# Feeding the first pair of experts: one-hot products of token tiles in SBUF in place of an indirect DMA

## The chip, the cores and the metric

The kernel runs on one core of one Trainium2 chip. The metric is the device time of one execution in microseconds (us), median of three runs. A difference of about 0.2% (3.9 us) is what a measurement of this kernel can tell from no change.

## The reference

Two transformer blocks over 512 tokens of width 1024, all in fp32: feed-forward, mixer, feed-forward, then a second mixer and a mixture of experts. Only the last part is touched by the change:

```python
def hierarchical_moe(h, w_group, b_group, w_expert, b_expert, w_gate, w_up, w_down):
    ...
    g_sel = jnp.argmax(g_logits, axis=-1)               # 1 of 4 groups
    top_vals, top_idx = lax.top_k(e_in, TOP_K)          # 2 of its 8 experts
    weights = g_w[:, None] * jax.nn.softmax(top_vals, axis=-1)
    ...
    def expert_block(args):                             # each expert on its own tokens
        xb, e = args
        hid = jax.nn.silu(xb @ w_gate[e]) * (xb @ w_up[e])
        return hid @ w_down[e]
    ...
    y = jnp.sum(y_buf[dest].reshape(T, TOP_K, D) * weights[..., None].astype(h.dtype), axis=1)
```

There are 32 experts with 1024x512 gate and up matrices and a 512x1024 down matrix each, 192 MiB of weights in all, every byte of which is loaded once.

## The kernel before

The activations stand as eight tiles `xT[d]` of 128 features x 512 tokens. The MoE stage treats the experts as 16 pairs, each expert with 64 slots for tokens, so that a pair's tokens fill 128 columns. A pair needs 12 weight tiles of 1 MiB (`load_experts`, L1247): four for gate, four for up, four for down. All are issued on SP's queue in one fixed order into 18 buffers (`NWA` 9 on the right end of SBUF, `NWB` 9 on the left), so tile 18, the third tile of pair 0's down matrices, goes where pair 0's first gate tile was, and can be issued only when TensorE has read that one for the last time. The order is pair 0 gate, up, pair 1 gate, up, pair 0 down, pair 2 gate, and so on: tiles 18 and 19 wait for the first half of pair 0's gate, 20 and 21 for the second half, 22 to 25 for its up.

While the mixer's last products still run, `route_tile` (L1210) adds up the router's logits feature tile by feature tile, and `token_tile` (L1232) turns `xT[d]` into rows of tokens, four 128x128 transposes for each d, copied by ScalarE into `stage` (a tile `tok` for two d), and stored by a DMA on ScalarE's queue into `rows` in DRAM. `route` (L1313) finds the two experts of each token on VectorE and `pos`, the slot of each token in each expert. `route_weights` (L1355) makes the weights `Wb` from logits; in the list of work it comes later, and the planner mixes its operations into `route`.

`hot` (L1390) makes one-hot matrices `P[b]` (128 tokens x slots, bf16) by comparing slot numbers with `pos`. `fetch` (L1409) multiplies them with token numbers to learn which token sits in which slot, and `fetch_rows` (L1420) gathers those rows from DRAM by an indirect DMA on GpSimd's queue into a `tok` tile. `turned` (L1439) turns the gathered rows back, eight transposes for a pair, and VectorE multiplies with the norm's gain into `xe`. Before any expert runs, pairs 0 and 1 are fetched so.

`experts` (L1452) then runs a pair: `first(0, ..)` is the gate's product, `first(1, ..)` the up's, each of 16 matmuls for four of the eight feature tiles. For pair 0 TensorE's order is written out by hand (L1469 to L1479); for the later ones it is too, over the whole of `experts`:

```python
                self.turned(0, 0)
                first(0, range(4))
                self.turned(0, 1)
                first(0, range(4, 8))
                self.route_weights()
                self.scales(0)
                self.scales(1)
                self.hot(1)
                self.fetch(2)
                first(1, range(8))
```

Each engine works off its queue in order.

Of the kernel before, what the change touches and what calls it, by code (L numbers as in the profile page):

```python
# [7 lines left out]
F32 = mybir.dt.float32  # L8
F32R = mybir.dt.float32r
BF = mybir.dt.bfloat16  # L10
I32 = mybir.dt.int32
AF = mybir.ActivationFunctionType
OP = mybir.AluOpType
# [3 lines left out]
T = 512  # L17
# [252 lines left out]
class Kernel:  # L270
# [119 lines left out]
    def part(self, t, i, c0=0, c1=None):  # L390

        c1 = T - 128 * i if c1 is None else c1
        o = 512 * PART[i] + OFF[i]
        return t[:, o + c0:o + c1]
# [837 lines left out]
    def token_tile(self, d):  # L1232


        nc = self.nc
        if d % 2 == 0:
            self.stage = self.p_tok.tile([128, 4, 256], F32, name="tok", tag="tok")
        pt = self.z([128, 4, 128])
        for b in range(4):
            nc.tensor.transpose(pt[:, b], self.xT[d][:, b * 128:b * 128 + 128], self.ident)  # L1240
        o = 128 * (d % 2)
        nc.scalar.copy(self.stage[:, :, o:o + 128], pt)
        if d % 2:
            to = self.rows.rearrange("(b p) c -> p b c", p=128)[:, :, 128 * d - 128:128 * d + 128]
            nc.scalar.dma_start(to, self.stage)

    def load_experts(self, n):  # L1247

# [20 lines left out]
    def moe_begin(self, st):  # L1269
        nc = self.nc  # L1270
        P = lambda n, b=1, **k: self.pool(st, n, b, **(k or dict(side="right", reuse_waits="tile")))
        self.p_one, self.p_tok = P("one_moe"), P("tok", 3)
        self.fill(self.p_one, 64)
        self.p_we = [P("we_a", NWA)]
        self.we, self.n_we = {}, 0
        self.c_con2 = self.one([128, self.aps["con2"].shape[1]], "c_con2")
        nc.scalar.dma_start(self.c_con2, self.aps["con2"])
        self.w_r = self.wk(288).rearrange("p (d c) -> p d c", d=ND)
        nc.scalar.dma_start(self.w_r, self.aps["w_r"])
        self.b_r = self.one([128, 36], "b_r")  # L1280
        nc.scalar.dma_start(self.b_r, self.aps["b_r"].to_broadcast([128, 36]))
        self.tri = self.one([128, 256], "tri", BF)
        nc.gpsimd.memset(self.tri, 1.0)
        nc.gpsimd.affine_select(self.tri[:, :128], self.tri[:, :128], [[1, 128]], OP.is_gt, 0.0, base=0, channel_multiplier=-1)
        self.top = self.one([128, 4, 8], "top")
        self.tb = self.one([128, 4, 2], "tb", BF)
        nc.vector.tensor_copy(self.tb.rearrange("p b c -> p (b c)"), self.con2("parts"))
        self.rows = P("rows", space=bass.MemoryType.DRAM).tile([T, D], F32, name="rows")
        self.acc = self.p_s1.tile([128, T], F32, name="acc")
        self.pr = self.at([128, 4, 36])  # L1290

    def moe(self, st):
        P = lambda n, b=1: self.pool(st, n, b, reuse_waits="tile")
        self.p_xe, self.p_sel, self.p_o = P("xe", 4), P("sel"), P("oexp")
        self.p_we += reversed([P(f"we_b{i}") for i in range(NWB)])
        self.load_experts(192)
        with self.hp():
            self.route()
        self.ws, self.xg = {}, {}
        with self.hp():  # L1300
            for pr in range(2):
                self.hot(0, 2 * pr, 2)
                self.fetch(pr)
        self.later = None
        for pr in range(16):
            if pr >= MAN:
                with self.tc.manual_schedule(engines={mybir.EngineType.PE}):
                    self.experts(pr)
            else:
                self.experts(pr)  # L1310
        self.overflow()
# [75 lines left out]
        nc.vector.tensor_copy(Wb[:, :, 2:9:3], r)  # L1387
        nc.vector.tensor_copy(self.Wb[:, :, :, 9:], self.tb[:, :, None, :].to_broadcast([128, 4, 16, 2]))

    def hot(self, g, first=0, n=4):  # L1390

        nc = self.nc
        if first == 0:
            self.P = [self.p_sel.tile([128, 256], BF, name=f"P{b}") for b in range(4)]
        s = [128, n, 64]
        for b in range(4):
            e = 4 * g + first
            nc.vector.tensor_tensor(self.P[b][:, 64 * first:64 * first + 64 * n].rearrange("p (e s) -> p e s", e=n),
                                    self.con2("slots")[:, None, :].to_broadcast(s),
                                    self.pos[:, b, e:e + n, None].to_broadcast(s), op=OP.is_equal)  # L1400

    def slots(self, pr, cols, n):

# [5 lines left out]
    def fetch(self, pr):  # L1409

        nc = self.nc
        ws = self.ws[pr] = self.p_sel.tile([128, 32], F32, name="ws", bufs=4)
        p = self.slots(pr, self.tb, 2) if pr < 2 else self.slots(pr, self.Wb[:, :, pr], 11)
        n = 0 if pr < 2 else 9
        nc.vector.tensor_reduce(ws[:, 2:3], p[:, n:n + 2], AX.X, OP.add)
        self.fetch_rows(pr, ws)
        if pr > 1:
            self.scales(pr, p)

# [18 lines left out]

    def turned(self, pr, half):  # L1439

        nc = self.nc
        if half == 0:
            self.xe = []
        p = self.at([128, 4, 128])
        for k in range(4):
            c = 512 * half + 128 * k
            nc.tensor.transpose(p[:, k], self.xg[pr][:, c:c + 128], self.ident)
        t = self.p_xe.tile([128, 4, 128], F32, name="xe", tag="xe")
        nc.vector.tensor_tensor(t, p, self.vec("norm2", 4 * half, 4)[:, :, None].to_broadcast([128, 4, 128]), op=OP.mult)
        self.xe += [t[:, k] for k in range(4)]  # L1450

    def experts(self, pr):  # L1452

        nc = self.nc
# [6 lines left out]
        def first(kind, kk):  # L1461
            for k in kk:
                for e in range(2):
                    c = 512 * (k % 4)
                    mm(gu[kind][64 * e:64 * e + 64], self.xe[k][:, 64 * e:64 * e + 64], w(kind, k // 4, e)[:, c:c + 512],  # L1465
                       start=(k == 0), stop=(k == 7))

        if pr == 0:
            with self.tc.manual_schedule(engines={mybir.EngineType.PE}):  # L1469
                self.turned(0, 0)  # L1470
                first(0, range(4))
                self.turned(0, 1)
                first(0, range(4, 8))
                self.route_weights()
                self.scales(0)
                self.scales(1)
                self.hot(1)
                self.fetch(2)
                first(1, range(8))  # L1479
            self.overflow_count()  # L1480
        else:
            first(0, range(8))
            first(1, range(8))
            if pr < 14:
                self.fetch(pr + 2)
# [65 lines left out]
        if last:  # L1551


            part = lambda: self.p_xe.tile([128, T], F32R, name="xe", tag="xe")
            with self.hp():
                down(0, part(), part(), self.mm())
            v[1] = part(), part()
            held = {d: self.z() for d in range(4, 8)}
            for c in TAIL.split():
                n = int(c[1])  # L1560
# [152 lines left out]
```

## Time and profile before

| | us |
|---|---|
| median of three runs (1925.04 to 1925.8) | 1925.8 |
| the profiled execution: its own time | 1927.15 |
| its span, first to last instruction | 1925.3 |
| PE busy in the span | 1863.8 (97%) |
| DVE, ACT, POOL busy | 901.8, 643.9, 307.7 |
| mean granted TensorE clock | 0.988 |

Times in the rows are us from the span's start. PE is TensorE's matmuls, DVE VectorE, ACT ScalarE, POOL GpSimd, SP the engine on whose queue the weights are issued. The MoE stage is the last quarter, from about 1426 us on.

### The profile page before, as it was taken

The numbers are of one execution on the slowest core, as the hardware profiler recorded it, in microseconds if no ns is written. First come the engines' busy times: TensorE is split into PE (matmuls) and PEld (weight loads), VectorE is DVE, ScalarE is ACT, GpSimd is POOL, SyncE is SP. The second block draws the span as 40 slices with busy tenths as digits, with TensorE's granted clock in tenths as the row PEclk, the third lists the DMA queues.
The fourth block names the chain that finished last, engine by engine and source line by source line (L and its number), as shares of the span: only waits on it lengthen the run. The fifth ranks groups of instructions, "written<-read, shape, count | busy, mean of one in ns | idle before, by whom it ended". The sixth has DMA issues, their size and how long they took to land.

```text
span 1925.3 us, 22975 instructions
## 1 busy us (share of the span) xinstructions
PE 1863.8 (97%) x8605; PEld 1305.7 (68%) x8605; DVE 901.8 (47%) x1734; ACT 643.9 (33%) x1218; POOL 307.7 (16%) x290
## 2 busy tenths in 40 slices
PE   8999999999999999999999999999978999999998
PEld 6888888877666778888888888777762333333333
DVE  5444453344998745444443343456651333343232
ACT  5333333344445734333333333466520100000000
POOL 3322210133021032222320100012120000000000
PEclk9999999999999999999999999999988999999999
DMA  4222232222111122222222222211297999999997
GB/s 155 99 99 97 92 102 99 97 79 71 66 56 44 45 88 99 88 99 99 99 99 98 91 99 90 86 55 54 89 404 290 420 419 420 420 420 419 419 421 282
DMA packets 69185, 330.49 MB, mean 172 GB/s; under 512 B 8784, under 2 KB 11216, under 8 KB 45008
## 3 DMA queue, kind: packets, MB, share of 16 engines
q1 hardware_dynamic: 63648, 321.48, 43.4%
q0 software_dynamic: 2304, 4.20, 0.6%
q10 hardware_dynamic: 3120, 3.32, 0.6%
q8 instruction: 69, 1.13, 0.2%
q14 instruction: 44, 0.36, 0.1%
HBM read 328.97 MB, written 4.19 MB: 173 GB/s over the span
## 4 chain that ended last, share of the span: by engine, by line
PE 60%; DMA 6%; DVE 3%; ACT 2%; issue 1%; POOL 0%; ACTq 0%; POOLq 0%; SPq 0%; DVEq 0%
PE mm L429 11%; PE mm L431 11%; PE mm L430 11%; PE mm L1465 8%; DMA we<-in_w_moe 5%; PE z L1521 4%; PE z L1539 1%; PE z L450 1%; PE z L452 1%; PE z L451 1%; PE z L918 1%; PE z L1538 1%; PE at L1179 1%; PE z L877 1%; DVE wk L1515 1%
## 5 line engine op out<-in xcount | busy, mean ns | idle before, releaser
L252 DVE TENSOR_TENSOR wl<-raw,wh 128x512 fp32r<-128x512 f32 x440 | 347.9, 792 | 442.1 <-ACT wh L251 432.9
L251 ACT CAST wh<-raw 128x512 fp32r<-128x512 f32 x440 | 272.4, 622 | 557.7 <-PE mm L430 468.5
L429 PE MATMUL mm<-xs,wh 128*128 128x512 f32 x1008 | 396.7, 394 | 7.3 <-ACT wh L251 7.3
L431 PE MATMUL mm<-xs,wl 128*128 128x512 f32 x1008 | 394.9, 392 | 1.0 <-DVE wl L252 1.0
L430 PE MATMUL mm<-xs,wh 128*128 128x512 f32 x1008 | 394.8, 392 | 0.6 <-DVE xs L502 0.4
L1465 PE MATMUL mm<-we,xe 128*64 128x512 f32 x1024 | 232.6, 602 | 2.6 <-DMA we<-in_w_moe 1.2
L429 PEld LDWEIGHTS mm<-xs,wh 128*128 128x128 f32 x1008 | 189.6, 188 | 54.2 <-ACT wh L251 7.3
L430 PEld LDWEIGHTS mm<-xs,wh 128*128 128x128 f32 x1008 | 189.6, 188 | 47.5 <-issue 5.7
L431 PEld LDWEIGHTS mm<-xs,wl 128*128 128x128 f32 x1008 | 189.6, 188 | 44.0 <-issue 4.1
L1465 PEld LDWEIGHTS mm<-we,xe 128*64 128x64 f32 x1024 | 73.7, 138 | 148.6 <-issue 136.3
L429 PE MATMUL mm<-hid,wh 128*128 128x512 f32 x352 | 136.9, 389 | 0.0
L430 PE MATMUL mm<-hid,wh 128*128 128x512 f32 x352 | 136.9, 389 | 0.0
L431 PE MATMUL mm<-hid,wl 128*128 128x512 f32 x352 | 136.9, 389 | 0.0
L563 POOL TENSOR_TENSOR wk<-wk 128x512 f32<-128x512 f32 x44 | 69.9, 1591 | 310.1 <-DVE wk L562 292.5
L1521 PE MATMUL z<-we,wk 128*64 128x512 f32 x480 | 113.8, 599 | 2.6 <-DMA we<-in_w_moe 2.3
L1514 ACT ACTIVATE oh<-z,ws 128x512 fp32r<-128x512 f32 x30 | 20.6, 688 | 247.4 <-PE z L1521 247.4
L1493 DVE SCALAR_TENSOR_TENSOR wk<-mm,ws,wk 128x512 f32<-128x512 f32 x16 | 12.0, 751 | 182.0 <-issue 160.6
L513 POOL TENSOR_TENSOR acc<-acc,wd 128x512 f32<-128x512 f32 x34 | 46.5, 1367 | 270.3 <-ACT wd L512 269.6
L1545 DVE TENSOR_TENSOR x<-z,x 128x512 f32<-128x512 f32 x116 | 72.0, 683 | 20.6 <-PE z L1539 20.6
L1426 POOL DMA_INDIRECT tok<-rows,islot x16 | 16.1, 1006 | 388.0 <-DVE islot L1424 324.2
L1521 PEld LDWEIGHTS z<-we,wk 128*64 128x64 f32 x480 | 32.6, 136 | 63.9 <-issue 54.3
L429 PEld LDWEIGHTS mm<-hid,wh 128*128 128x128 f32 x352 | 66.1, 188 | 13.8
(441 smaller groups left out, 2529.8 us busy)
## 6 DMA issues: line engine op xcount, KB each, us to landing
we<-in_w_moe SPq DMA_DIRECT2D x188, 1024.0 KB, 19.9
raw<-in_stream SPq DMA_DIRECT2D x220, 512.0 KB, 3.2
we<-in_w_moe SPq DMA_DIRECT2D x16, 256.0 KB, 9.8
x<-in_xT SPq DMA_DIRECT2D x8, 256.0 KB, 6.0
rows<-tok ACTq DMA_DIRECT2D x4, 512.0 KB
out<-x SPq DMA_DIRECT2D x8, 256.0 KB, 2.3
c_con<-in_con SPq DMA_DIRECT2D x1, 512.0 KB
c_con<-in_con ACTq DMA_DIRECT2D x1, 344.0 KB
```

What stands on the lines that cost most here:

```text
L251: nc.scalar.copy(h, r)
L252: nc.vector.tensor_sub(l, r, h.bitcast(F32))
L429: mm(p, h, xh[k], start=(k == 0), stop=False)
L430: mm(p, h, xl[k], start=False, stop=False)
L431: mm(p, l, xh[k], start=False, stop=(k == n - 1))
L450: mm(pv[b], self.xh[k][:, t], wh, start=(k == 0), stop=False)
L513: nc.gpsimd.tensor_add(self.acc, self.acc, sq)
L563: nc.gpsimd.tensor_mul(u, s, u)
L1465: mm(gu[kind][64 * e:64 * e + 64], self.xe[k][:, 64 * e:64 * e + 64], w(kind, k // 4, e)[:, c:c + 512], start=(k == 0), stop=(k == 7))
L1514: nc.scalar.activation(oh, pd, AF.Copy, scale=ws[:, 0:1])
L1521: mm(p[64 * e:64 * e + 64], ht[:, k * 128 + 64 * e:k * 128 + 64 * e + 64], self.down_rows(w(2, half, e), half, k), start=(k == 0), stop=(k ...
L1545: nc.vector.tensor_add(self.xT[d], p, self.xT[d])
```

## The change

Pair 0 no longer fetches its rows. `token_tile` keeps all four stage tiles in SBUF (`tok` now has four buffers). `hot_first` makes fp32 one-hots `P0[b]` for the first two experts in a `wk` tile; `gather_first` multiplies each 128x128 block of the stage tiles with them, four matmuls (one for each block of tokens) for each of the eight feature tiles, 32 in all, and `gained` takes the place of the second half of `turned`. Pair 0's token numbers are still found (`fetch(0)`, without the DMA), later. Pairs 1 and up are fetched as before. `hot(0)` is made once for four experts. All operations of `route_weights` on VectorE are put behind the last operation of `hot(0)`, and the two `scales` now stand ahead of the gate's second half in TensorE's order. `xe` has two buffers in place of four; the last pair's outputs go to `tok` tiles instead.

```diff
@@ -1234,15 +1234,15 @@
 
         nc = self.nc
         if d % 2 == 0:
-            self.stage = self.p_tok.tile([128, 4, 256], F32, name="tok", tag="tok")
+            self.stage.append(self.p_tok.tile([128, 4, 256], F32, name="tok", tag="tok"))
         pt = self.z([128, 4, 128])
         for b in range(4):
             nc.tensor.transpose(pt[:, b], self.xT[d][:, b * 128:b * 128 + 128], self.ident)
         o = 128 * (d % 2)
-        nc.scalar.copy(self.stage[:, :, o:o + 128], pt)
+        nc.scalar.copy(self.stage[-1][:, :, o:o + 128], pt)
         if d % 2:
             to = self.rows.rearrange("(b p) c -> p b c", p=128)[:, :, 128 * d - 128:128 * d + 128]
-            nc.scalar.dma_start(to, self.stage)
+            nc.scalar.dma_start(to, self.stage[-1])
 
     def load_experts(self, n):
 
@@ -1269,8 +1269,8 @@
     def moe_begin(self, st):
         nc = self.nc
         P = lambda n, b=1, **k: self.pool(st, n, b, **(k or dict(side="right", reuse_waits="tile")))
-        self.p_one, self.p_tok = P("one_moe"), P("tok", 3)
-        self.fill(self.p_one, 64)
+        self.p_one, self.p_tok = P("one_moe"), P("tok", 4)
+        self.fill(self.p_one, 96)
         self.p_we = [P("we_a", NWA)]
         self.we, self.n_we = {}, 0
         self.c_con2 = self.one([128, self.aps["con2"].shape[1]], "c_con2")
@@ -1283,6 +1283,7 @@
         nc.gpsimd.memset(self.tri, 1.0)
         nc.gpsimd.affine_select(self.tri[:, :128], self.tri[:, :128], [[1, 128]], OP.is_gt, 0.0, base=0, channel_multiplier=-1)
         self.top = self.one([128, 4, 8], "top")
+        self.stage = []
         self.tb = self.one([128, 4, 2], "tb", BF)
         nc.vector.tensor_copy(self.tb.rearrange("p b c -> p (b c)"), self.con2("parts"))
         self.rows = P("rows", space=bass.MemoryType.DRAM).tile([T, D], F32, name="rows")
@@ -1291,16 +1292,15 @@
 
     def moe(self, st):
         P = lambda n, b=1: self.pool(st, n, b, reuse_waits="tile")
-        self.p_xe, self.p_sel, self.p_o = P("xe", 4), P("sel"), P("oexp")
+        self.p_xe, self.p_sel, self.p_o = P("xe", 2), P("sel"), P("oexp")
         self.p_we += reversed([P(f"we_b{i}") for i in range(NWB)])
         self.load_experts(192)
         with self.hp():
             self.route()
         self.ws, self.xg = {}, {}
         with self.hp():
-            for pr in range(2):
-                self.hot(0, 2 * pr, 2)
-                self.fetch(pr)
+            self.hot_first()
+            self.hot(0)
         self.later = None
         for pr in range(16):
             if pr >= MAN:
@@ -1387,17 +1387,47 @@
         nc.vector.tensor_copy(Wb[:, :, 2:9:3], r)
         nc.vector.tensor_copy(self.Wb[:, :, :, 9:], self.tb[:, :, None, :].to_broadcast([128, 4, 16, 2]))
 
-    def hot(self, g, first=0, n=4):
-
-        nc = self.nc
-        if first == 0:
-            self.P = [self.p_sel.tile([128, 256], BF, name=f"P{b}") for b in range(4)]
-        s = [128, n, 64]
-        for b in range(4):
-            e = 4 * g + first
-            nc.vector.tensor_tensor(self.P[b][:, 64 * first:64 * first + 64 * n].rearrange("p (e s) -> p e s", e=n),
-                                    self.con2("slots")[:, None, :].to_broadcast(s),
-                                    self.pos[:, b, e:e + n, None].to_broadcast(s), op=OP.is_equal)
+    def hot(self, g):
+
+        nc = self.nc
+        P = []
+        s = [128, 4, 64]
+        for b in range(4):
+            t = self.p_sel.tile(s, BF, name=f"P{b}")
+            last = nc.vector.tensor_tensor(t, self.con2("slots")[:, None, :].to_broadcast(s),
+                                           self.pos[:, b, 4 * g:4 * g + 4, None].to_broadcast(s), op=OP.is_equal)
+            P.append(t.rearrange("p e s -> p (e s)"))
+        self.P = P
+        self.last_hot = last
+
+    def hot_first(self):
+
+        nc = self.nc
+        t = self.wk()
+        s = [128, 2, 64]
+        self.P0 = [t[:, 128 * b:128 * b + 128] for b in range(4)]
+        for b in range(4):
+            nc.vector.tensor_tensor(self.P0[b].rearrange("p (e s) -> p e s", e=2), self.con2("slots")[:, None, :].to_broadcast(s),
+                                    self.pos[:, b, 0:2, None].to_broadcast(s), op=OP.is_equal)
+
+    def gather_first(self, kk):
+
+        nc = self.nc
+        for k in kk:
+            if k % 4 == 0:
+                self.pg = self.at([128, 4, 128])
+            o = 128 * (k % 2)
+            for b in range(4):
+                nc.tensor.matmul(self.pg[:, k % 4], self.stage[k // 2][:, b, o:o + 128], self.P0[b], start=(b == 0), stop=(b == 3))
+            if k % 4 == 3:
+                self.gained(self.pg, k // 4)
+
+    def gained(self, p, half):
+        if half == 0:
+            self.xe = []
+        t = self.p_xe.tile([128, 4, 128], F32, name="xe", tag="xe")
+        self.nc.vector.tensor_tensor(t, p, self.vec("norm2", 4 * half, 4)[:, :, None].to_broadcast([128, 4, 128]), op=OP.mult)
+        self.xe += [t[:, k] for k in range(4)]
 
     def slots(self, pr, cols, n):
 
@@ -1413,7 +1443,8 @@
         p = self.slots(pr, self.tb, 2) if pr < 2 else self.slots(pr, self.Wb[:, :, pr], 11)
         n = 0 if pr < 2 else 9
         nc.vector.tensor_reduce(ws[:, 2:3], p[:, n:n + 2], AX.X, OP.add)
-        self.fetch_rows(pr, ws)
+        if pr:
+            self.fetch_rows(pr, ws)
         if pr > 1:
             self.scales(pr, p)
 
@@ -1438,16 +1469,11 @@
 
     def turned(self, pr, half):
 
-        nc = self.nc
-        if half == 0:
-            self.xe = []
         p = self.at([128, 4, 128])
         for k in range(4):
             c = 512 * half + 128 * k
-            nc.tensor.transpose(p[:, k], self.xg[pr][:, c:c + 128], self.ident)
-        t = self.p_xe.tile([128, 4, 128], F32, name="xe", tag="xe")
-        nc.vector.tensor_tensor(t, p, self.vec("norm2", 4 * half, 4)[:, :, None].to_broadcast([128, 4, 128]), op=OP.mult)
-        self.xe += [t[:, k] for k in range(4)]
+            self.nc.tensor.transpose(p[:, k], self.xg[pr][:, c:c + 128], self.ident)
+        self.gained(p, half)
 
     def experts(self, pr):
 
@@ -1467,13 +1493,17 @@
 
         if pr == 0:
             with self.tc.manual_schedule(engines={mybir.EngineType.PE}):
-                self.turned(0, 0)
+                self.gather_first(range(4))
+                self.fetch(1)
+                self.gather_first(range(4, 5))
                 first(0, range(4))
-                self.turned(0, 1)
-                first(0, range(4, 8))
-                self.route_weights()
+                self.gather_first(range(5, 8))
+                self.fetch(0)
+                with self.tc.issue_after(self.last_hot.ins):
+                    self.route_weights()
                 self.scales(0)
                 self.scales(1)
+                first(0, range(4, 8))
                 self.hot(1)
                 self.fetch(2)
                 first(1, range(8))
@@ -1551,10 +1581,10 @@
         if last:
 
 
-            part = lambda: self.p_xe.tile([128, T], F32R, name="xe", tag="xe")
+            part = lambda: [t[:, i] for t in [self.p_tok.tile([128, 2, T], F32R, name="tok", tag="tok")] for i in range(2)]
             with self.hp():
-                down(0, part(), part(), self.mm())
-            v[1] = part(), part()
+                down(0, *part(), self.mm())
+            v[1] = part()
             held = {d: self.z() for d in range(4, 8)}
             for c in TAIL.split():
                 n = int(c[1])
```

## Rows read from the trace of the kernel before

**Rows 1.** Page, part 2: DMA busy in tenths, 40 slices of 48 us.

```profile
DMA  4222232222111122222222222211297999999997
```

**Rows 2.** Windows: busy us (instructions) by engine, granted clock, DMA share, GB/s.

```profile
1396.00:1442.00 46.00, 37.81 (x223) 32.63 (x221) 27.30 (x86) 13.58 (x25) 10.13 (x8) 0.85 1.02 419
1442.00:1457.50 15.50, 7.31 (x27) 2.96 (x28) 0.72 (x2) 0.00 (x0) 2.22 (x2) 0.58 0.19 57
1457.50:1469.00 11.50, 10.05 (x54) 3.74 (x54) 5.55 (x22) 1.97 (x2) 0.99 (x1) 0.85 0.95 370
1469.00:1472.00 3.00, 3.00 (x18) 1.01 (x14) 0.00 (x0) 0.00 (x0) 0.00 (x0) 1.00 0.56 148
1472.00:1893.00 421.00, 407.01 (x1868) 159.23 (x1862) 138.64 (x287) 36.88 (x58) 12.89 (x13) 1.00 1.01 420
```

**Rows 3.** Waits of PE from 1700 to the end: total us, times, longest.

```profile
PE z L1521 <- DMA we<-in_w_moe: 2.3, 2, 1.3
...
PE mm L1465 <- DMA we<-in_w_moe: 1.2, 1, 1.2
```

**Rows 4.** Timeline of PE: start, us, instruction, count, [idle before, releaser].

```profile
1435.99 1.60 PE L1406 MATMUL z<-tb,P 128*128 128x2 bf16 x8 [0.71 <-DVE P L1398]
1449.40 1.11 PE L1447 MATMUL at<-c_con,tok 128*128 128x128 f32 x4 [11.81 <-DMA tok<-rows,islot]
1451.30 5.54 PE L1465 MATMUL mm<-we,xe 128*64 128x512 f32 x16 [0.78 <-DVE xe L1449]
...
1458.22 3.65 PE L1465 MATMUL mm<-we,xe 128*64 128x512 f32 x16 [0.35 <-DVE xe L1449]
1461.80 0.36 PE L1406 MATMUL z<-Wb,P 128*128 128x9 bf16 x8
...
1464.52 2.02 PE L1465 MATMUL mm<-we,xe 128*64 128x512 f32 x6
```

**Rows 5.** Timeline of SP: the first weight issues after the pause.

```profile
1456.87 0.80 SPq L1261 DMA_DIRECT2D we<-in_w_moe  x2
...
1461.89 0.80 SPq L1261 DMA_DIRECT2D we<-in_w_moe  x2
...
1469.89 0.33 SPq L1261 DMA_DIRECT2D we<-in_w_moe  x1
```

**Rows 6.** Timeline of POOL: the first indirect DMA.

```profile
1444.99 1.23 POOL L1426 DMA_INDIRECT tok<-rows,islot  x1 [15.88 <-DMA rows<-tok]
```

**Rows 7.** Timeline of DVE: routing, one-hots, weights.

```profile
1432.51 0.17 DVE L1365 TENSOR_REDUCE gw<-ge 128x4 f32<-128x16 f32 x1 [1.19 <-ACT ge L1363]
...
1435.32 0.29 DVE L1352 SCALAR_TENSOR_TENSOR pos<-z,ab 128x128 f32<-128x128 f32 x1 [0.21 <-PE z L1349]
1435.64 1.71 DVE L1398 TENSOR_TENSOR P<-c_con,pos 128x128 bf16<-128x128 f32 x8
...
1441.51 0.36 DVE L1387 CAST Wb<-wk 128x192 bf16<-128x192 f32 x1
...
1462.93 1.42 DVE L1398 TENSOR_TENSOR P<-c_con,pos 128x256 bf16<-128x256 f32 x4
```

**Rows 8.** Timeline of PE: 128x128 transposes (L1240) and fp32 products (L1075).

```profile
1388.73 3.15 PE L1075 MATMUL z<-U,R 128*128 128x129 f32 x20
1391.72 2.40 PE L1075 MATMUL z<-V,R 128*128 128x128 f32 x20
...
1429.25 3.65 PE L1240 MATMUL z<-c_con,x 128*128 128x128 f32 x16
```

**Rows 9.** Windows, as rows 2: the granted clock around small products and transposes.

```profile
1388.70:1390.20 1.50, 1.50 (x9) 1.50 (x8) 0.51 (x1) 0.69 (x1) 0.00 (x0) 0.50 0.98 336
1390.40:1391.90 1.50, 1.50 (x16) 1.50 (x15) 0.60 (x2) 0.25 (x2) 0.00 (x0) 1.00 0.01 3
...
1429.00:1433.00 4.00, 3.91 (x19) 3.50 (x18) 2.16 (x16) 1.91 (x5) 0.12 (x1) 0.50 1.03 428
1449.40:1455.00 5.60, 4.81 (x14) 1.95 (x16) 0.69 (x1) 0.00 (x0) 0.00 (x0) 0.50 0.09 34
```

## The prediction

> **What bounds the kernel now.** I read the DMA line of the page first [rows 1]: its last quarter is one block at full share with a notch at its head. Windows cut along that block [rows 2] show the weight stream full from 1396 to 1442 us, nearly idle to 1457.5 (share 0.19), then 0.95 and 0.56 to 1472, and full again, 420 GB/s at a share of 1.01, to 1893. In that last stretch PE is busy 407 of 421 us as well, so the question is which of the two sets the end. The waits of PE from 1700 on [rows 3] answer it: only 3.5 us in all, but for weights. So the stream sets the end, and PE would be ready only some 3.5 us sooner. The idle time of the DMA engines is 0.81 x 15.5 + 0.05 x 11.5 + 0.44 x 3 = 12.6 + 0.6 + 1.3 = 14.5 us, and nothing later gives it back.
>
> Its cause is on PE [rows 4]: it stands still for 11.81 us, until 1449.40, for the gathered rows of pair 0. These were asked for only at 1444.99, since the indirect DMA waited for the store of the rows [rows 6], which lay behind the full stream. All 18 weight buffers are full by then, and the next weights are issued at 1456.87, as the first half of pair 0's gate ends at 1456.84 [rows 4, 5]. The pairs 1461.89 and 1469.89 follow PE in the same manner.
>
> **Part by part.** *Route without weights between.* VectorE stood 1.19 us for an exponential of the weights, then did 0.17 us of them, before the router went on [rows 7]. Behind the last one-hot these are off the path: `pos`, done at 1435.61, comes about 1.2 us sooner, 1434.4. If the planner keeps the gap, this is 0.
>
> *One-hots.* Eight 128x128 took 1.71 us, 0.21 each [rows 7]. Four in fp32: 0.9 us, the first at 1434.7, the last at 1435.3. No row shows a fp32 output of this compare; at the 0.29 of `pos`, also fp32 and 128 wide, it is 0.3 us more, hidden behind the products. The four 128x256 of `hot(0)` take 1.42 us [rows 7] to 1436.7, under PE's products.
>
> *Products.* 16 transposes of 128x128 took 3.65 us at half clock, 0.228 each; 20 fp32 products of the same shape took 2.40 us at full clock, 0.12 each [rows 8, 9]. I price a product so at either clock. The first 16 run from 1434.7 to 1438.4. They read the first two stage tiles, which are copied while the mixer's products still run, and wait for no DMA. Then VectorE's `xe`: from the transposes' end at 1450.51 to the first expert matmul at 1451.30 is 0.79 us [rows 4], so 1439.2; meanwhile PE does the four small matmuls of `fetch(1)` and four products more (0.5 to 0.9 us), to 1439.4. The experts start at 1439.4 in place of 1451.30.
>
> [...]
>
> *Gate, first half.* 16 matmuls took 5.54 us where the clock rose on the way and 3.65 where it was full [rows 4, 9]; all at half clock would be 7.3. So it ends at 1443.05, 1444.95 or 1446.7, against 1456.84. Which it is hangs on the clock. [...]
>
> [...]
>
> *Restart of the stream.* 0.65 us behind that matmul [rows 2, 5]: 1443.7, 1445.6 or 1447.4, against 1457.5. Tiles 18 and 19 take 2.5 us each at 420 GB/s, and pair 1's gather 1.25 us (128 rows of 4 KB, 0.52 MB), to about 1450.0. By then the second half must be through: 12 products 1.45 us, `xe` 0.8 (under it the slots of `fetch(0)` and both `scales`, 0.2 to 0.4 us), 16 matmuls 3.65: 1443.05 + 5.9 = 1448.95. It is, so tiles 20 and 21 follow at once, and the up (3.65 per half, to 1452.6) is again ahead of tile 22. The idle after 1442 shrinks to 1.7 us; 0.4 of this is filled as before, by the rest of the store (0.19 x 15.5 = 2.9 us of work, less two gathers of 1.25). So 1.3 is left.
>
> *The wait that is added.* `scales(0)` and `scales(1)` now stand in PE's queue ahead of the gate's second half and the up, and need `Wb`. VectorE's work for it is 4.4 us in rows of 0.16 to 0.36, which ran to 1441.87 [rows 7]; from 1436.7 on, with `xe` and reductions between, it ends near 1443.5, and PE comes to it at 1444.5. Hidden, with 1 us to spare. `hot(1)` is now made behind the gate's second half, which takes away the gap of 1.9 us ahead of the up (second half's end 1461.87 to 1464.52 less the slots) [rows 4].
>
> *Moves with one answer.* The indirect DMA of pair 0 goes (0.52 MB, 1.25 us of stream); that of pair 1 stays behind the store, issued near 1445 as the first was [rows 6]; it took 4.4 us to land with the stream idle (to 1449.40), twice that with it full is my estimate, 1454, and it is wanted after the up, at 1456 or later. `xe` in two buffers costs nothing: TensorE has read a pair's `xe` through before it turns the next. The tail's `tok` tiles are free by then. The pools shift by 4 KB, so early weight tiles may wait for other tiles; the stream may fill up to 2.5 us (one tile) later or sooner, of which 1.3 us lies in idle time.
>
> **The sum.** Idle 14.5 becomes 1.3, traffic falls by 1.25: -14.5 with the quick gate; -12.6 with the 5.54, -10.8 at half clock throughout. PE's own path moves further: the up ended at 1464.52 + 7.3 = 1471.8 or later [rows 4] and would end at 1456.3, 15.5 us sooner or more, so PE doesn't become the bound; it waits some 3 us more for weights at the end. I take -13.2, between the first two. The profiled execution has a span of 1925.3 in 1927.15; it would be 1912.1 in 1913.95, and the median of 1925.8 becomes 1912.6.
>
> **Rivals.** *VectorE's queue.* If the planner puts all of `route_weights` ahead of the first `xe` (4.4 us plus two waits on ScalarE's exponentials, 1436.7 to 1441.7), the gate starts at 1442.5 and its half ends at 1448.0 with the 5.54; the stream restarts at 1448.7, idle 6.3: 14.5 - 6.3 + 1.25 = 9.5 less, 1916.3. For it: strict order, and the mix that the planner made before [rows 7]. Against: `xe` stands first in the list. [...] *Not what it says.* The idle goes, but PE or a new pause gives it back: pair 1's rows come late, or the early tiles slip by many. With 1.2 us of gain left, that is 1924.6. Against: the 15.5 us by which PE is ahead. [...]
>
> **How the numbers follow.** Forecast (gain of 10.5 to 15) 0.74; VectorE's queue 0.11, dear products 0.03; a gain between that and 4 us 0.04; not what it says 0.04; slower 0.04. The range leaves out the last three: from 1910.3 (-15.5, nearly all idle and the gather gone) to 1919.0 (the queue rival with one early tile lost). Faster by over 0.2% (3.9 us, about what a measurement can tell from no change) 0.92, within 0.04, slower 0.04.
>
> **What would show it.** In the changed profile: no wait of PE for `tok` ahead of the first gate matmul, which starts near 1439.4; 16 products in 2 to 3.7 us; clock 1.00 before 1445; the first issue after the pause at 1443 to 1445; a DMA share of 1.0 from there to 1880; more waits of PE for weights after 1700. Wrong it would be if the first gate matmul starts after 1445, if `scales` holds PE for `Wb`, or if the stream pauses again before 1480.

## The result, and the profile after

The changed kernel takes 1906.12 us (median of 5, 1905.23 to 1906.98), the kernel before beside it 1925.8: ratio 0.9899, 95% interval 0.9884 to 0.9913, or 19.7 us less. The forecast was 1912.6 in a range from 1910.3 to 1919.0. The sign and the main mechanism were right, the size was not: 6.5 us more came than were reckoned, and the range was missed on the fast side. The profiled execution has a span of 1904.3 in 1906.03, against 1925.3 in 1927.15; the differences of traces below are against that span, 21.0 us longer. One execution of e8 below took 7267.5 us at a granted clock of 0.454 and is left out of its row.

Page, part 2, of the kernel after (DMA busy in tenths, 40 slices): the notch of [rows 1] at the head of the last block is gone.

```profile
DMA  4222232222111112222222232211199999999997
```

Windows of the kernel after, with the columns of [rows 2]. The first five answer [rows 2] (the stream's last landing is now at 1872), the others show the clock, as [rows 9] did.

```profile
1396.00:1442.00 46.00, 44.26 (x272) 37.81 (x271) 26.08 (x79) 12.22 (x23) 9.10 (x7) 0.93 0.99 386
1442.00:1457.50 15.50, 15.00 (x99) 6.91 (x99) 7.18 (x26) 2.39 (x3) 2.22 (x2) 1.00 0.93 358
1457.50:1469.00 11.50, 11.50 (x56) 4.65 (x54) 0.03 (x1) 0.85 (x2) 0.00 (x0) 1.00 1.01 425
1469.00:1472.00 3.00, 3.00 (x18) 1.03 (x16) 0.89 (x2) 0.00 (x0) 0.00 (x0) 1.00 1.03 434
1472.00:1872.00 400.00, 387.70 (x1784) 154.47 (x1780) 136.91 (x285) 35.55 (x56) 12.86 (x13) 1.00 1.01 425
1425.00:1428.50 3.50, 3.50 (x18) 3.26 (x17) 2.69 (x19) 1.65 (x3) 0.50 (x1) 0.53 1.02 431
1428.50:1430.60 2.10, 0.44 (x8) 0.24 (x7) 1.56 (x12) 0.68 (x2) 0.00 (x0) 1.00 0.99 417
1430.70:1432.70 2.00, 2.00 (x14) 2.00 (x15) 2.00 (x9) 0.01 (x1) 0.00 (x0) 0.76 0.98 404
1432.70:1434.70 2.00, 2.00 (x11) 2.00 (x11) 1.79 (x11) 0.50 (x2) 0.00 (x0) 0.50 1.03 424
1434.70:1437.10 2.40, 2.40 (x23) 2.32 (x22) 2.28 (x8) 0.00 (x0) 0.00 (x0) 0.91 0.99 353
1437.20:1440.70 3.50, 3.50 (x17) 1.01 (x16) 0.40 (x3) 0.00 (x0) 0.00 (x0) 1.00 0.94 303
```

From 1442 to 1457.5 the share is 0.93 where it was 0.19, and in the windows from there on to 1872 it is above 1. The second thing to see is the last column: 425 GB/s in the long stretch, where [rows 2] have 420.

Timeline of PE, kernel after (start, us, instruction, count, [idle before, releaser]); it answers [rows 4].

```profile
1429.59 0.32 PE L1348 MATMUL z<-ab,tri 128*128 128x32 bf16 x6 [1.03 <-DVE ab L1343]
...
1430.67 5.47 PE L1421 MATMUL at<-wk,tok 128*128 128x128 f32 x32 [0.71 <-DVE wk L1410]
...
1436.08 1.14 PE L1421 MATMUL at<-wk,tok 128*128 128x128 f32 x8
1437.15 3.65 PE L1491 MATMUL mm<-we,xe 128*64 128x512 f32 x16
1440.73 2.94 PE L1421 MATMUL at<-wk,tok 128*128 128x128 f32 x24
...
1444.46 3.65 PE L1491 MATMUL mm<-we,xe 128*64 128x512 f32 x16 [0.50 <-DVE xe L1429]
...
1448.34 7.09 PE L1491 MATMUL mm<-we,xe 128*64 128x512 f32 x32
```

The wait of 11.81 us for `tok` is gone; the first gate matmul starts at 1437.15 where it was 1451.30, and the gate's first half takes 3.65 us at full clock. There are 16 products in the first group by the code, and 32 records: each product leaves two.

Timelines of SP, VectorE and POOL, kernel after: the issues behind the first gate half ([rows 5]), the routing chain ([rows 7]), the first indirect DMA ([rows 6]).

```profile
1440.83 0.80 SPq L1261 DMA_DIRECT2D we<-in_w_moe  x2
...
1448.14 0.80 SPq L1261 DMA_DIRECT2D we<-in_w_moe  x2
1452.02 0.80 SPq L1261 DMA_DIRECT2D we<-in_w_moe  x2
```

```profile
1430.00 0.29 DVE L1352 SCALAR_TENSOR_TENSOR pos<-z,ab 128x128 f32<-128x128 f32 x1 [0.47 <-PE z L1349]
1430.33 0.90 DVE L1410 TENSOR_TENSOR wk<-c_con,pos 128x128 f32<-128x128 f32 x4
1431.14 1.43 DVE L1397 TENSOR_TENSOR P<-c_con,pos 128x256 bf16<-128x256 f32 x4
...
1436.18 0.69 DVE L1429 TENSOR_TENSOR xe<-at,c_vec 128x512 f32<-128x512 f32 x1
...
1437.24 0.36 DVE L1387 CAST Wb<-wk 128x192 bf16<-128x192 f32 x1
```

```profile
1444.18 1.23 POOL L1457 DMA_INDIRECT tok<-rows,islot  x1 [18.68 <-PE z L1436]
```

Waits of PE from 1700 to the end, kernel after ([rows 3]; only one line names weights):

```profile
PE z L1551 <- DMA we<-in_w_moe: 1.9, 2, 1.3
```

**Where the 21 us come from.** The last weights land 20.9 us sooner (1892.97 to 1872.10), and the tail behind them is as long as it was. From 1472 to there the kernel before moves 421 us x 420 GB/s = 176.8 MB, the kernel after 400 x 425 = 170.0 MB. The 6.8 MB less are 16.0 us at 425 GB/s: more landed before 1472, and one gather (0.52 MB) fell away. The rest, 176.8 MB at 425 in place of 420 GB/s, is 4.9 us: a faster stream, which no term of the forecast had.

The earlier bytes have two places. Windows around the restart, first of the kernel before, then of the kernel after:

```profile
1380.00:1396.00 16.00, 13.19 (x78) 11.01 (x77) 11.41 (x29) 9.79 (x37) 4.22 (x5) 0.89 0.50 176
1396.00:1436.00 40.00, 36.33 (x216) 31.80 (x214) 21.69 (x61) 13.58 (x25) 10.13 (x8) 0.90 1.02 421
1436.00:1472.00 36.00, 21.85 (x100) 8.54 (x102) 11.89 (x49) 1.97 (x2) 3.21 (x3) 0.69 0.60 223
```

```profile
1380.00:1396.00 16.00, 13.52 (x89) 11.12 (x89) 11.66 (x28) 9.92 (x33) 3.26 (x6) 1.00 0.79 284
1396.00:1436.00 40.00, 38.26 (x234) 34.45 (x233) 24.49 (x74) 12.22 (x23) 9.10 (x7) 0.91 1.00 404
1436.00:1472.00 36.00, 35.50 (x206) 15.94 (x205) 9.69 (x34) 3.24 (x4) 2.22 (x2) 1.00 0.96 371
```

Between 1436 and 1472 the kernel after moves 371 GB/s x 36 us = 13.4 MB against 223 x 36 = 8.0: 5.3 MB, or 12.5 us. That is the pause, as forecast. From 1380 to 1436 it moves 20.7 MB against 19.7, some 2.5 us. That is 1.7 MB more up to 1396, because the stream starts sooner, less 0.7 MB behind it, where the kernel after moves 404 GB/s and the kernel before 421; e4 below shows that this loss comes with the pools. Timelines of SP there, first of the kernel before, then of the kernel after:

```profile
1382.46 0.33 SPq L1261 DMA_DIRECT2D we<-in_w_moe  x1
1387.74 0.33 SPq L241 DMA_DIRECT2D raw<-in_stream  x1
1392.67 0.33 SPq L1261 DMA_DIRECT2D we<-in_w_moe  x1
```

```profile
1381.65 0.33 SPq L1261 DMA_DIRECT2D we<-in_w_moe  x1
1386.40 0.33 SPq L241 DMA_DIRECT2D raw<-in_stream  x1
1388.56 0.81 SPq L1261 DMA_DIRECT2D we<-in_w_moe  x2
```

The weights stand in one queue with the mixer's last load (L241), which waits for the mixer; they follow it 4.9 us later before and 2.2 us later after, and all of it comes 1.3 us sooner. Nothing in the diff touches the mixer.

### The profile page after: what moved, and what is told of

Read it like the earlier page. It is cut to its first block, busy times and chain, and to the rows that moved or that the text cites. A ratio compares the mean times of both kernels' runs of the same rounds, so it can differ in the third digit from the quotient of the medians.

```text
span 1904.3 us, 23089 instructions
## 1 busy us (share of the span) xinstructions
PE 1861.4 (98%) x8661; PEld 1312.1 (69%) x8661; DVE 900.4 (47%) x1733; ACT 644.4 (34%) x1218; POOL 306.3 (16%) x289
## 4 chain that ended last, share of the span: by engine, by line
PE 84%; DVE 7%; DMA 4%; ACT 2%; issue 2%; POOL 0%; POOLq 0%; DVEq 0%; ACTq 0%; SPq 0%
PE mm L429 17%; PE mm L430 17%; PE mm L431 17%; PE mm L1491 9%; PE z L1551 5%; DMA we<-in_w_moe 4%; PE z L1569 2%; PE z L450 2%; PE z L452 2%; PE z L451 2%; PE z L1568 1%; DVE wk L859 1%; DVE wk L1545 1%; PE at L1179 1%; PE z L431 1%
## 5 line engine op out<-in xcount | busy, mean ns | idle before, releaser
L431 PE MATMUL mm<-xs,wl 128*128 128x512 f32 x1008 | 395.4, 393 | 1.0 <-DVE wl L252 1.0
L1491 PE MATMUL mm<-we,xe 128*64 128x512 f32 x1024 | 226.6, 594 | 0.7 <-DVE xe L1429 0.5
L431 PEld LDWEIGHTS mm<-xs,wl 128*128 128x128 f32 x1008 | 190.1, 189 | 44.3 <-issue 4.1
L431 PE MATMUL mm<-hid,wl 128*128 128x512 f32 x352 | 136.9, 389 | 0.0
L431 PEld LDWEIGHTS mm<-hid,wl 128*128 128x128 f32 x352 | 66.1, 188 | 13.8
```

Of the source, the lines that this page charges most:

```text
L431: mm(p, l, xh[k], start=False, stop=(k == n - 1))
```

## The experiments

Two questions: what is each part of the change worth (products, weights behind the one-hots, the other pools), and what makes the stream faster. Each kernel ran beside the kernel before, whose median was between 1925.6 and 1926.2 in all of them. "Rate" is that of all DMA traffic between 1480 and 1860 us; in the kernel after, 158.2 of its 161.5 MB are on the queue of the weights. A filler, `fill(pool, n)`, takes n bytes of every partition that nothing reads or writes, and so shifts the addresses of other tiles.

| kernel | us (range) | ratio, 95% | rate, GB/s |
|---|---|---|---|
| after | 1906.1 (1905.2–1907.0) | 0.9884–0.9913 | 425 |
| e2, weights not behind | 1910.1 (1908.4–1911.4) | 0.9901–0.9934 | 425 |
| e3, weights behind only | 1922.4 (1920.8–1925.2) | 0.9975–0.9994 | 420 |
| e4, layout only | 1923.4 (1922.6–1925.1) | 0.9977–0.9996 | 425 |
| e5, filler 64 | 1911.5 (1910.0–1913.1) | 0.9911–0.9944 | 420 |
| e8, products twice | 1912.3 (1910.3–1913.6) | 0.9913–0.9952 | 425 |
| e10, filler 96 only | 1921.2 (1919.2–1922.8) | 0.9967–0.9986 | 425 |
| e11, scales last | 1908.2 (1906.6–1909.0) | 0.9892–0.9922 | 425 |

**The kernel before, a second time (e1).** No edit. 

> The kernel before, unchanged, for a second profile beside the others of this call. Why: the changed kernel's weight stream runs at 425 GB/s from 1480 to 1860 us, before's at 420, and over some 170 MB that is 4.8 us that no step of the prediction had. If the rate belongs to the chip or the day, this profile shows 425 GB/s; if it belongs to the kernel (layout of the pools, or what is in flight), it shows 420 again and a span near 1925.

It took 1926.65 us, again at 420 GB/s and with a wait of 13.3 us for `tok`. The rate belongs to the kernel, not to the execution.

**Without the weights behind (e2), and that alone on the kernel before (e3).**

```diff
-                with self.tc.issue_after(self.last_hot.ins):
-                    self.route_weights()
+                self.route_weights()
```

> The changed kernel with route_weights not put behind the one-hots; all else as after. Compiled, its mixer's last heads stand in before's order on TensorE, while after's stand in another. Theory A (this one line replanned the mixer, which is why the router came 3.7 us sooner, and it also saves the gap in the route): pos comes some 5 us later than in after, the stream's pause is some 4 to 5 us longer, 1910 to 1911 us. Theory B (the mixer's new order is worth nothing; the 4 us come from the layout): 1907.3, the 1.2 us of the route alone. The rate stays 425 GB/s by either, since the layout is after's.

> The kernel before with route_weights put behind the last one-hot, and nothing else: pair 0 is still fetched by indirect DMA. Compiled, its mixer has after's order. Theory A: the router and the start of the weight stream move 4 us, and the end with them, 1920 to 1922 us, with the pause of the stream as long as before (some 15 us, PE waits over 11 us for tok). Theory B: at most the 1.2 us of the route, and those are lost in the wait for the rows: 1925 to 1926. Rate 420 GB/s if the layout sets it.

In e2 the line is worth 1910.05 - 1906.12 = 3.9 us (the intervals of the ratios overlap, the ranges of the times don't), in e3, where the kernel before gets it (with `last_hot` kept in `hot`), 1925.8 - 1922.4 = 3.4. The forecast had 1.2, for a shorter chain from the router to `pos`. That is there: from the start of the router's last matmuls (L1222) to `pos` it is 1431.71 - 1425.10 = 6.6 us in e2 and 1430.00 - 1424.06 = 5.9 after. Ahead of it, the router itself starts 1.0 us sooner, and that lies in the mixer. These 1.7 us are what the traces place of the line: the two profiled executions differ by 2.4 us (1908.39 and 1906.03), not by the 3.9 of the medians. Waits of PE between 1230 us and the one-hots, first of the kernel before, then of the kernel after:

```profile
PE z L918 <- DVE R L1190: 2.4, 2, 1.3
PE z L1084 <- DVE x L1081: 1.0, 1, 1.0
PE z L1084 <- ACT R L919: 0.4, 1, 0.4
```

```profile
PE z L1084 <- DVE x L1081: 1.3, 1, 1.3
PE z L918 <- DVE R L1190: 0.9, 2, 0.7
```

e1, e2, e4 and e10, without the line, show 2.4 us at L918; after, e3, e8 and e11, with it, 0.9. The order of TensorE's instructions in the mixer's last heads differs between the compiled programs with and without the line, and is the same within each kind. So the planner (which orders each engine's instructions when the kernel is built), given one constraint more behind the router, has planned the work ahead of it otherwise. The mixer ends sooner, and the weights that share its queue start sooner: 1387.32 in e3, 1388.56 after, against 1390.07 in e2, 1391.91 in e1 and 1393.14 in e4. Which of the planner's steps does it was not followed.

**The pools without the products (e4).** Token pool 4, `xe` pool 2, filler 96, the tail's halves in `tok`; all else as before. 

> The kernel before with after's pools alone: tok 4, xe 2, the filler 96, and the last pair's outputs in tok tiles. The work and the mixer's order are before's. Theory C (the layout sets the rate of the weight stream): 425 GB/s from 1480 to 1860 us, and 1921 us. Theory D (the rate comes from something else, such as how many weight DMAs are in flight when TensorE is far ahead): 420 GB/s and 1925 to 1926 us. Early weight tiles may start up to 2.5 us sooner or later by either.

2.4 us less at a rate of 425 GB/s: the rate comes with the pools. Of the 4.9 us that it is worth only half shows, and the wait for `tok` is 14.7 us in this trace, against 11.8 and 13.3 in the two of the kernel before. Windows from 1410 to 1436 us of e10 (below: of these edits the filler alone), of e4 and of the kernel after show a loss:

```profile
1410.00:1436.00 26.00, 23.76 (x152) 21.72 (x150) 12.23 (x43) 6.94 (x13) 7.21 (x6) 0.87 1.02 423
1410.00:1436.00 26.00, 23.86 (x155) 21.60 (x153) 12.97 (x45) 7.09 (x14) 7.82 (x7) 0.85 1.00 398
1410.00:1436.00 26.00, 24.26 (x157) 22.46 (x157) 13.96 (x60) 5.81 (x11) 4.24 (x4) 0.87 1.00 392
```

Every kernel with the new pools moves 381 to 398 GB/s there, the four without them (before, e1, e3, e10) 416 to 423. The 25 GB/s between e4 and e10 are 0.65 MB, or 1.5 us of the stream. SP issues no weight for 20.0 us in e4 (1404.69 to 1424.64), 12.9 of them in one wait for the mixer's last products (L431); in e10 it stands for 14.6 (1406.61 to 1421.23). So early weight tiles do come later with the shifted pools, as the prediction allowed; that this is the whole of the difference between e4 and e10 was not tested. From e4 to e2, both at 425 GB/s and without the line, is 13.35 us for the products, the new order of PE and the gather that falls away.

**The filler back to 64 (e5), and 96 alone (e10).**

```diff
-        self.fill(self.p_one, 96)
+        self.fill(self.p_one, 64)
```

> The changed kernel with the MoE filler back at 64: the nine weight buffers at the right end of SBUF then start 32 bytes off a multiple of 64 (131360), as in before (135456), and nothing else moves. Theory E (these 32 bytes set the rate of the weight stream): 420 GB/s from 1480 to 1860 us, and some 4.8 us more than after, 1910 to 1911 us. Theory F (the rate hangs on the other changes of the layout, the 4 KB or the number of tok and xe buffers): 425 GB/s and 1906.

> The kernel before with one line changed: the filler at the right-hand pool is 96 instead of 64 bytes, so that all eighteen weight buffers lie at multiples of 64; token tiles, xe tiles, products and order are those of before. Theory E: 425 GB/s instead of 420 between 1480 and 1860 us, and so up to 5 us less before anything is given back: 1921 if the pause of the DMA engines keeps its length, 1923.5 if the pause grows as it did in e4 (PE's wait for the first tokens 14.7 us there against 13.3). Theory T (the fourth token tile or the tail's buffers made e4's rate): 420 GB/s and 1925.8.

32 bytes of filler cost the kernel after 5.4 us, and give the kernel before 4.4 (1921.2 beside 1925.6). Nothing else differs, so the filler is the cause of the rate, and e10 is a gain in itself: one number, without the products.

DMA of e5 and of e10, each from 1480 to 1860 us:

```profile
DMA packets 23241, 159.50 MB, mean 420 GB/s; under 512 B 3435, under 2 KB 3435, under 8 KB 4137
```

```profile
DMA packets 23586, 161.43 MB, mean 425 GB/s; under 512 B 3510, under 2 KB 3510, under 8 KB 4283
```

**Which addresses.** The filler moves the nine right-hand weight buffers and the token tiles above them. Eight kernels (the kernel after with other fillers, as in the next table) tell them apart; the offsets are of the first buffer of each half, and the others follow at 8192 bytes.

```diff
         self.p_one, self.p_tok = P("one_moe"), P("tok", 4)
         self.fill(self.p_one, 96)
+        self.fill(P("gap"), 32)
...
         self.p_xe, self.p_sel, self.p_o = P("xe", 2), P("sel"), P("oexp")
+        self.fill(self.p_o, 32)
```

The first added line, with 32, 64 or 128, moves the right-hand buffers alone (e12, e14, e15; e13 has it with a filler of 64, which moves the token tiles alone); the second moves the left-hand ones (e9; e6 and e16, with 32 and 128, have it with a filler of 64). e7 has fillers of 352 and 384.

| kernel | left, past a multiple of 256 | right, past a multiple of 256 | rate | us (range) |
|---|---|---|---|---|
| before | 128 | 32 | 420 | 1925.8 |
| e5 | 128 | 32 | 420 | 1911.5 (1910.0–1913.1) |
| e6 | 160 | 32 | 420 | 1910.1 (1909.4–1912.2) |
| e12 | 128 | 224 | 420 | 1910.6 (1909.0–1912.4) |
| e14 | 128 | 192 | 421 | 1911.2 (1908.8–1913.2) |
| e15 | 128 | 128 | 421 | 1909.9 (1909.0–1910.5) |
| after | 128 | 0 | 425 | 1906.1 (1905.2–1907.0) |
| e13, token tiles off | 128 | 0 | 425 | 1906.9 (1904.9–1907.0) |
| e9 | 160 | 0 | 425 | 1907.2 (1905.1–1907.8) |
| e16 | 0 | 32 | 424 | 1908.5 (1907.6–1910.0) |
| e7 | 0 | 0 | 426 | 1906.1 (1905.5–1906.5) |

> The changed kernel with all 18 weight buffers 32 bytes off a multiple of 64: filler 64 on the right, 32 bytes more on the left. Theory E: the loss doubles with the number of buffers off, 415 GB/s from 1480 to 1860 us and 1915 to 1916 us. Theory F: 425 GB/s and 1906.

> The changed kernel with all 18 weight buffers at multiples of 512 bytes (before this, those on the left are at 128 past a multiple of 512, those on the right at 0 or 256). If finer alignment is worth as much again, 430 GB/s and 1901; if 64 bytes are all that counts, 425 GB/s and 1906.

> The changed kernel with the nine left-hand weight buffers moved by 32 bytes (to 32 past a multiple of 64) and the nine right-hand ones, with the token tiles, left at multiples of 64. e5 moved the right-hand buffers and the token tiles and cost 5.4 us; e6 moved all eighteen and cost no more (4.0 us). Theory E (half of the stream's buffers off a multiple of 64 is enough, whichever half): weight stream 420 GB/s between 1480 and 1860 us, 1910 to 1912. Rival T (what costs is the token tiles, or something else on the right that moves with them): 425 GB/s and 1906.

> The changed kernel with a gap of 32 bytes between the token tiles and the nine right-hand weight buffers: those buffers start at 131296 (32 past a multiple of 64), the token tiles stay where they are in the changed kernel (205056, a multiple of 64). Theory W (the right-hand weight buffers make the rate): 420 GB/s between 1480 and 1860 us, 1910 to 1912. Rival T (the token tiles make it): 425 GB/s, 1906.

> The changed kernel with the filler at 64 and the 32 bytes put below the token tiles: the token tiles start at 205088 (32 past a multiple of 64, as in the kernel before), the right-hand weight buffers at 131328 as in the changed kernel. Theory W: 425 GB/s, 1906. Rival T: 420 GB/s, 1910 to 1912. If both e12 and e13 show 425, it takes the two together; if both show 420, either is enough.

> The changed kernel with a gap of 64 bytes below the token tiles: the right-hand weight buffers start at 131264, a multiple of 64 but not of 128. If a multiple of 64 is enough: 425 GB/s between 1480 and 1860 us, 1906. If it takes 128 or 256: below 425, at 420 (1910 to 1912) where any offset costs the same.

> The changed kernel with a gap of 128 bytes: the right-hand weight buffers start at 131200, a multiple of 128 but not of 256. If 64 or 128 is enough: 425 GB/s, 1906. If it takes 256: 420 GB/s, 1910 to 1912. The left-hand ones stood 128 past a multiple of 256 in every kernel at 425 but e7, so I lean to 425.

> The changed kernel with the filler at 64 (right-hand weight buffers at 131360, 32 past a multiple of 256, as in e5) and 128 bytes below the left-hand ones (56064, a multiple of 256). Theory R (the right-hand half alone matters): 420 GB/s between 1480 and 1860 us, 1910 to 1912, as e5. Theory O (one half of the buffers on a multiple of 256 is enough, whichever): 425 GB/s, 1906.

DMA of the kernel after, of e15, of e16 and of e7, each from 1480 to 1860 us:

```profile
DMA packets 23570, 161.46 MB, mean 425 GB/s; under 512 B 3512, under 2 KB 3512, under 8 KB 4241
```

```profile
DMA packets 23274, 159.85 MB, mean 421 GB/s; under 512 B 3426, under 2 KB 3426, under 8 KB 4127
```

```profile
DMA packets 23517, 161.01 MB, mean 424 GB/s; under 512 B 3506, under 2 KB 3506, under 8 KB 4250
```

```profile
DMA packets 23640, 161.90 MB, mean 426 GB/s; under 512 B 3520, under 2 KB 3520, under 8 KB 4265
```

Three theories fell on the way. That each buffer off the grid costs its share: e6 and e5 cost the same, and e9 nothing. That the token tiles do it: e12 against e13. That a multiple of 64 is enough, which the expectations up to e13 speak of: e14 and e15 are at 421. What the rows bear out is this: with neither half at a multiple of 256 bytes the stream runs at 420 to 421 GB/s, with one half there, either, at 424 to 425, with both at 426. How far off the right half lay made no difference: 32, 128, 192 and 224 all gave 420 to 421. e16 stood against the theory that only the right-hand half counts: its rate is 424, and its time lies between the two groups. For the left half alone e16 is the only kernel. For both halves e7 is, and its buffers are at multiples of 512 as well, where those of the others at a multiple of 256 are not; so its last 1 GB/s may come from the second half or from the 512. Why one half is nearly enough stays open; the trace shows no single transfer's time within a full queue.

**The products twice (e8).**

```diff
+            for again in range(2):
-            for b in range(4):
-                nc.tensor.matmul(...)
+                for b in range(4):
+                    nc.tensor.matmul(...)
```

Each column block is summed twice in turn, and the second sum stands. 

> The changed kernel with each of pair 0's one-hot products made twice (64 in place of 32, same output). In after's profile the 32 take 5.47 + 1.14 + 2.94 us of PE, 0.25 to 0.33 each. If they lie on the path to the weight stream, 20 more before the first half of the gate delay its end by some 5 to 5.5 us and 12 more that of the second half by 3 more; the stream had 1.7 us of idle time in after, and the store of the rows fills part of the pause, so the end moves by 5 to 8.5 us: 1911 to 1914.5. If the stream's pause is set by the store or something else, less than 2 us.

Timeline of PE in e8:

```profile
1429.09 7.41 PE L1422 MATMUL at<-wk,tok 128*128 128x128 f32 x64 [0.71 <-DVE wk L1410]
...
1438.40 3.65 PE L1492 MATMUL mm<-we,xe 128*64 128x512 f32 x16
1441.99 5.62 PE L1422 MATMUL at<-wk,tok 128*128 128x128 f32 x48
```

32 products more cost 1912.3 - 1906.1 = 6.2 us, 0.19 each, of the order of their time on PE: 7.41 us for 32 products at full clock, 0.23 each. The price is rough: e8's three times lie 4.1 to 7.5 us above 1906.1, and in its trace the mixer ends 1.6 us sooner and the clock stays at 1.00 through the first 32 products, where it is 0.76, 0.50 and 0.91 in the first 16 of the kernel after. But it is far from the "less than 2 us" of the rival. They lie on the path that sets the end, and so do the change's own.

**Scales behind the gate's second half (e11).** `first(0, range(4, 8))` is written ahead of `route_weights` and the two `scales`, as in the kernel before. 

> The changed kernel with one statement moved: the second half of the first gate's products is written ahead of the route weights and scales, as in the kernel before, not behind them. The change put the scales there, and the prediction counted that at nothing, with PE's room of 1 us. Theory 'hidden': same within 0.2% (1902.5 to 1910), PE's gate products then end at most a microsecond sooner. Rival: PE sits in scales for the weights of the route (they end at 1437.6 us there), the weights' next issue is later by that, and the move gains 1 to 3 us (1903 to 1905).

Waits of PE in e11 from 1380 to 1460:

```profile
PE z L1436 <- DVE P L1397: 1.5, 3, 1.2
```

1908.2 against 1906.1, with intervals that overlap (0.9892 to 0.9922 and 0.9884 to 0.9913). The trace gives a reason for a small loss: behind the gate, the slots must wait 1.5 us for the one-hots of `hot(1)`, and the up behind them takes 8.78 us where the kernel after needs 7.09; the granted clock from 1436 to 1472 us is 0.95 in e11 and 1.00 in the kernel after. So the move counted at nothing costs nothing, and is, if anything, the better order.

## Why the prediction was right and wrong

In medians, along the kernels that share a part: the pools 1925.8 to 1923.4 (e4), 2.4 us; the products 1923.4 to 1910.05 (e2), 13.35; the weights behind 1910.05 to 1906.12, 3.9. The forecast had 0, 12.0 and 1.2. So of the 6.5 us that were missing, 5.1 lie outside of the gather and 1.35 in it.

*What bounds the kernel:* right. The stream sets the end, and the notch was what it lost. The idle after 1442 was forecast at 1.3 us and is 0.07 x 15.5 = 1.1; the pause was forecast to give back 13.2 with the gather apart, and between 1436 and 1472 it gave 12.5. PE's share moved as reckoned: the up ends at 1455.4 (forecast 1456.3). But PE does not wait 3 us more for weights at the end; it waits 1.9 us from 1700 on, less than the 3.5 of [rows 3], since the stream came forward by as much as PE and 5 us besides. By this wait the two are nearly level now. e7's 426 GB/s bought no more time, but the 1.1 us that they are worth would hardly show in ranges of 1 to 2 us.

*"The pools shift by 4 KB ... may fill up to 2.5 us (one tile) later or sooner":* this is the step that failed most. The term was bounded by when tiles come free, taken as nothing in the sum, and the price of where they lie was left out. That price measured 4.9 us in the trace, 5.4 in e5 and 4.4 in e10. The slip that the term did name came too, as a loss of about 1.5 us by the bytes (e4 against e10), and the pools as a whole gained 2.4 in e4. With the filler back at 64 (e5), the kernel takes 1911.5, inside the range and 1.1 us from the forecast; that it comes so near is luck, for there the other errors partly cancel.

*"Route without weights between", 1.2 us:* mis-sized. The chain itself shrank by 0.7 (e2 against after). The rest of the 3.9 and 3.4 of e2 and e3 comes with the mixer's end as far as the traces place it (1.0 us at the router in e2, 2.4 us in all between the two profiled executions); I took that end as fixed because no line of it was edited. An edit that gives the planner a constraint can move any work that it plans together with it.

*Products, 0.228 at half and 0.12 at full clock:* wrong by the count. The 20 records of L1075 in [rows 8] are 10 products (the loops around that line run 1 + 2 + 3 + 4 times), while a transpose leaves one record (the four of `turned(0, 0)` in [rows 4] leave four). Read so, [rows 8] give 0.24 at full clock, and the trace after has 12 products in 2.94 us, 0.245, at full clock, and 16 in 5.47, 0.34, at a clock of 0.76, 0.50 and 0.91. The first 16 took 1.8 us more than the 3.65 forecast. It was hidden by `pos`, which came 4.1 us sooner than the forecast's 1434.4: the gate started at 1437.15, not 1439.4. By luck, two errors of opposite sign left the end of the gate's first half only 2.3 us ahead (1440.80 against 1443.05), and the first weight issue with it, at 1440.83. The gate has the same two records a matmul: by the loops of `first` half of it is 8 matmuls (four feature tiles, two experts), not 16 as the kernel's description and the prediction have it. It was priced as a group, so no sum hung on that.

The chances of "dear products" (0.03) and of "slower" (0.04) are those of a product that costs more than in the sum. No run shows a price that would make either of them; measured are 0.23 to 0.245 us at full clock, and 0.34 in the first 16, where the sum had 0.228.

*Clock:* right. It was 0.53 during the transposes (1425 to 1428.5), full in the gate from its first matmul, and the gate's half took the 3.65 us. In the first products it went 0.76, 0.50, 0.91, so "clock 1.00 before 1445" holds. That the gate would be quick was an estimate of mine, and what raises the clock is not shown: it was already at 1.00 from 1428.5 to 1430.6, behind the transposes, while PE was busy for 0.44 of 2.1 us, fell in the products, and rose again before they ended.

*The wait that is added, `scales` for `Wb`:* right, no wait of PE for `Wb` is in the trace. `Wb` is done at 1437.60, long before the 1443.5 reckoned, since all of `route_weights` but its last two operations stands ahead of the first `xe` at 1436.18, which is the rival "VectorE's queue" in nearly its full form. It cost nothing, for the 16 products were not done until 1436.1.

*Pair 1's gather:* right; it is issued at 1444.18 (forecast near 1445) and lands 5.4 us later, sooner than the estimate of twice 4.4, and PE waits for no tokens.

## What to carry to other kernels

Where a transfer stream sets the end, compute the start address of every buffer that it fills before and after an edit of the pools: 32 bytes of filler were worth a quarter of the whole change here, and e10 gets them with one number. Undo each part of a change alone, the parts that should cost nothing first. And before a row's time is divided by its count, hold the count against the loops of the code.

## What the runs showed of the hardware

- The stream of weights in 8 KB rows (with the other 2% of DMA traffic) ran at 420 to 421 GB/s with no half of its 18 buffers at a multiple of 256 bytes in SBUF (six kernels of the table), at 425 with the right half there (three), at 424 with the left (one), at 426 with both, at multiples of 512 (one); 380 us each.
- A product of 128x128 by 128 columns in fp32 left two records (32 for 16) and took 0.23 to 0.245 us at full clock; a transpose of the same shape left one (four for the four of `turned` in [rows 4]).
- Behind the transposes, at 0.53, the granted clock rose to 1.00 in the kernel after while PE was busy for 0.44 of 2.1 us. The products that followed ran at 0.76, then 0.50, then 0.91, in the kernel after, and at 1.00 in e8, from 1429.1 to 1436.4 us; the first 16 took 5.47 us in the kernel after and 3.84 in e6.
